# A hand-written order for TensorE beside the RWKV scan, and 16-wide diagonal blocks with two merges on TensorE

## The chip, the core and the metric

The kernel runs on one core of one Trainium2 chip. The metric is the device time of one execution in microseconds (us). The core has five engines that run side by side, each working through its own list in order: TensorE (PE, matrix products, with weight loads as PEld), VectorE (DVE), ScalarE (ACT), GpSimd (POOL) and SyncE (SP), which here only issues DMA transfers.

## The reference, cut to what matters

One encoder layer for two sequences (1024 and 256 tokens, width 1024): attention (MLA) and a bidirectional RWKV-7 scan side by side, merged by gates, then a SwiGLU FFN. What the change touches is the scan, the gates and the attention's output projection:

```python
def wkv_scan(r, w, k, v, kk, a, reverse):
    def step(S, inp):
        r_t, w_t, k_t, v_t, kk_t, a_t = inp
        sa = jnp.einsum('bhvk,bhk->bhv', S, -kk_t)
        S = (S * w_t[:, :, None, :]
             + sa[..., :, None] * (kk_t * a_t)[..., None, :]
             + v_t[..., :, None] * k_t[..., None, :])
        y = jnp.einsum('bhvk,bhk->bhv', S, r_t)
        return S, y
...
        o_mla = mla_branch(p_mla, q_a_norm[l], kv_a_norm[l], w_uq[l], w_ukv[l]) @ w_mla_o[l]
        o_rwkv = rwkv_branch(p_rwkv, ...) @ w_rwkv_o[l]
        gm, gr = jnp.split(jax.nn.sigmoid(p_gate), 2, axis=-1)
        x = x + g1 * ((gm * o_mla + gr * o_rwkv) @ w_out[l])
```

## The kernel before, in words

The scan is computed in chunks. A *batch* is 128 tokens of one sequence in both directions at once, with 8 heads: ten batches (two of the short sequence, eight of the long one). Inside a batch there are two *steps* of 64 tokens. Per step, direction and head a 64x64 triangular system has to be solved; its inverse is built once per batch for all 32 systems. The functions, in `phase_rwkv`:

- `front` and `left` make a batch's scaled keys `bk` and left factors `lt` on VectorE, ScalarE and GpSimd from tiles `ld` that SP loads.
- `prepare` runs four `part`s per batch: products `pA` (the triangular matrices and their partners), copies of them by ScalarE into `aa`, `lt` and `arb`, masks by GpSimd, transposes `pT` into `bkt`; then `value_rows` transposes the values (`pv`). The PSUM pool `pa` has three buffers.
- `invert` (called by `solve`) builds the inverses. Diagonal blocks of 32 are inverted on VectorE by a chain of 31 elimination steps with two instructions each (`xt`, L865, and `W`, L867), between transposes (`X` L856, `dt` L869, `xr` L871). Two products per block pair on TensorE (`pw`, L877 and L882), with copies `aa` (L878, L879) and `tt` (L884, L885) after each, merge the 32-blocks to 64.
- `step` is the serial part: products `py` (L913), copies `ru` (L916 on ScalarE, L917 on VectorE), `py` with the inverse `tt` (L919), copies `xv` (L920, L921), the state update `pS` (L925, L926), the outputs (L931) and their copies to `yt`.

Beside this chain `phase_fill` gives TensorE independent work, the *fill*: the gate products of nine column tiles over five 256-token pieces (weights from `w_in`, split into a high and a low half by `split_w`: ScalarE casts, GpSimd subtracts; kept in DRAM as `gw` for later pieces), and then the attention's output projection (`mla_out`). All its products are issued in `product` (L1041). Before, `phase_fill` was traced as a whole after the scan, and the compiler's scheduler set the order of every engine by priorities: a step's instructions lie 4000 places ahead of their place in the text (`HP`), a solve's 100 (`HI`), and where nothing of these was ready in its model of the time, fill went in. The order is fixed when the program is built; on the chip each engine follows it and waits where an operand is late.

After the scan, `join` and `merge` apply the scan's result (tile `or`, which takes the fill's buffer `x1`), and the FFN follows.

## Time and profile before

| | |
|---|---|
| time, median of 3 runs | 2687.57 us (2685.22 to 2699.12) |
| the profiled execution's own time | 2687.72 us |
| its span in the profile | 2686.0 us |
| TensorE / VectorE / ScalarE / GpSimd busy | 93% / 53% / 37% / 30% |
| mean granted clock of TensorE | 0.958 |

Busy shares are taken over the whole span. Instructions that only wait, issue DMAs or branch don't count as busy. The granted clock is a share of full speed: 1.00 is 2.4 GHz, 0.50 is 1.2 GHz. A product of f32 operands leaves two records in the profile, one in which the operands are fp32r leaves one.

### The profile page before, as it was taken

Reading aid. Unit: us, or ns where it says so; the run is one execution under the profiler, and the core shown is the slowest. Engines: PE = TensorE matmul, PEld = TensorE weight load, DVE = VectorE, ACT = ScalarE, POOL = GpSimd, SP = SyncE. Lnnn points to the kernel's source line nnn. Section 1 sums busy time; section 2 is a strip of 40 time slices with the busy share of each in tenths; the row PEclk is TensorE's granted clock in tenths of the full one; section 3 lists DMA queues with packets and bytes.
Section 4 is the critical chain, followed back from the end, with each engine's and each line's share of the span. In section 5 each row is a group of like instructions: output and inputs, shape, how many; then the busy total and the mean of one; then the engine's idle time right before and its main releaser. Section 6 shows DMA issues by size and latency. Waiting matters only on the chain.

```text
span 2686.0 us, 42442 instructions
## 1 busy us (share of the span) xinstructions
PE 2501.3 (93%) x17018; PEld 2121.5 (79%) x17018; DVE 1426.3 (53%) x2399; ACT 998.8 (37%) x1867; POOL 800.6 (30%) x789
## 2 busy tenths in 40 slices
PE   5999999989998799999898898899999999999997
PEld 3777777778887688888886677778888888888886
DVE  5655652357777688886785666552222232222328
ACT  4422332347676765555652233331110111101114
POOL 2112131021015655443434665442111111111123
PEclk7999999999999798899998999999999999999998
DMA  7654532100003545644656754221111111111113
GB/s 285 230 197 174 212 126 84 47 31 19 18 13 89 186 146 173 176 129 139 202 172 193 240 167 144 80 71 56 40 33 39 40 40 40 35 37 40 40 42 132
DMA packets 188470, 292.37 MB, mean 109 GB/s; under 512 B 16160, under 2 KB 106096, under 8 KB 188272
## 3 DMA queue, kind: packets, MB, share of 16 engines
q1 hardware_dynamic: 174880, 242.07, 28.4%
q0 software_dynamic: 5760, 26.22, 2.4%
q10 hardware_dynamic: 7632, 21.37, 2.3%
q8 instruction: 134, 2.20, 0.3%
q14 instruction: 64, 0.52, 0.1%
HBM read 211.95 MB, written 77.64 MB: 108 GB/s over the span
## 4 chain that ended last, share of the span: by engine, by line
PE 72%; DVE 16%; DMA 4%; issue 3%; POOL 2%; ACT 2%; SPq 0%; POOLq 0%; DVEq 0%; ACTq 0%
PE mm L67 43%; PE fp L1041 8%; PE s L627 3%; DVE xt L865 3%; DVE W L867 2%; PE o L661 2%; PE proj L560 2%; PE gps L453 2%; PE t L648 2%; PE pA L820 1%; PE py L913 1%; PE py L931 1%; PE ada_ps L170 1%; PE lora L369 1%; PE pS L925 1%
## 5 line engine op out<-in xcount | busy, mean ns | idle before, releaser
L55 POOL TENSOR_TENSOR wlo<-wraw,whi 128x1024 fp32r<-128x1024 f32 (+3 forms) x197 | 359.5, 1827 | 1168.0 <-ACT whi L53 1151.9
L53 ACT CAST whi<-wraw 128x1024 fp32r<-128x1024 f32 (+2 forms) x212 | 172.7, 818 | 917.3 <-issue 460.4
L67 PE MATMUL mm<-h2h,whi 128*128 128x512 f32 (+1 forms) x1056 | 279.5, 358 | 2.8 <-ACT whi L53 2.7
L67 PE MATMUL mm<-h2h,wlo 128*128 128x512 f32 (+1 forms) x1056 | 278.8, 358 | 2.7 <-POOL wlo L55 2.7
L67 PE MATMUL mm<-h2l,whi 128*128 128x512 f32 (+1 forms) x1056 | 278.3, 357 | 0.0
L67 PE MATMUL mm<-g,whi 128*128 128x512 f32 (+1 forms) x1056 | 240.7, 359 | 6.2 <-DVE ft L1251 5.6
L1041 PE MATMUL fp<-x,whi 128*128 128x256 f32 (+1 forms) x912 | 203.0, 316 | 15.0 <-ACT x L1023 8.3
L67 PEld LDWEIGHTS mm<-g,whi 128*128 128x128 f32 x1056 | 177.8, 190 | 38.0 <-issue 5.7
L67 PEld LDWEIGHTS mm<-h2h,whi 128*128 128x128 f32 x1056 | 177.2, 189 | 34.5 <-ACT whi L53 3.3
L67 PEld LDWEIGHTS mm<-h2h,wlo 128*128 128x128 f32 x1056 | 177.0, 189 | 34.3 <-POOL wlo L55 3.6
L67 PEld LDWEIGHTS mm<-h2l,whi 128*128 128x128 f32 x1056 | 177.1, 189 | 31.3 <-issue 0.5
L1263 DVE SCALAR_TENSOR_TENSOR x<-mm,g2h,x 128x512 f32<-128x512 f32 (+1 forms) x144 | 87.0, 656 | 196.3 <-PE mm L67 196.0
L1041 PEld LDWEIGHTS fp<-x,whi 128*128 128x128 f32 x912 | 153.5, 200 | 25.4 <-ACT x L1023 10.0
L1251 DVE SCALAR_TENSOR_TENSOR ft<-ft,mm 128x512 f32<-128x512 f32 (+1 forms) x66 | 36.0, 593 | 226.9 <-ACT ft L1250 226.9
L67 PE MATMUL mm<-hh,whi 128*128 128x512 f32 (+1 forms) x480 | 148.8, 368 | 6.9 <-ACT pp L320 3.9
L1041 PE MATMUL fp<-x,wlo 128*128 128x256 f32 (+1 forms) x456 | 144.4, 317 | 11.6 <-POOL wlo L55 7.6
L67 PE MATMUL mm<-hl,whi 128*128 128x512 f32 (+1 forms) x480 | 148.2, 365 | 7.0 <-DVE hl L265 6.9
L1252 DVE TENSOR_TENSOR ft<-ft,mm 128x512 f32<-128x512 f32 (+1 forms) x66 | 36.0, 593 | 217.5 <-PE mm L67 217.5
L67 PE MATMUL mm<-hh,wlo 128*128 128x512 f32 (+1 forms) x480 | 146.5, 365 | 0.0
L67 PE MATMUL mm<-g,wlo 128*128 128x512 f32 (+1 forms) x528 | 136.2, 359 | 1.2 <-POOL wlo L55 1.2
L865 DVE TENSOR_TENSOR xt<-W,X 128x126 f32<-128x126 f32 (+22 forms) x310 | 127.6, 412 | 9.0
L867 DVE TENSOR_TENSOR W<-W,xt 128x126 f32<-128x126 f32 (+22 forms) x310 | 125.0, 403 | 8.6
(320 smaller groups left out, 5210.7 us busy)
## 6 DMA issues: line engine op xcount, KB each, us to landing
wraw<-in_w_ffn_in_dram SPq DMA_DIRECT2D x56, 512.0 KB, 3.5
araw<-in_w_ada_dram ACTq DMA_DIRECT2D x32, 512.0 KB, 3.3
wraw<-in_w_ffn_out_dram SPq DMA_DIRECT2D x26, 512.0 KB, 3.6
wraw<-in_w_in_dram SPq DMA_DIRECT2D x20, 512.0 KB, 3.8
x<-scr_h SPq DMA_DIRECT2D x20, 512.0 KB, 7.7
whi<-scr_gw SPq DMA_DIRECT2D x36, 256.0 KB, 3.2
wlo<-scr_gw SPq DMA_DIRECT2D x36, 256.0 KB, 3.5
araw<-in_w_ada_dram SPq DMA_DIRECT2D x16, 512.0 KB, 9.4
```

Of the source, the lines that this page charges most:

```text
L53: nc.scalar.copy(hi, raw)
L55: (eng or nc.gpsimd).tensor_tensor(lo, raw, hi, ALU.subtract)
L67: nc.tensor.matmul(p[:, :n], lhsT=ww[:, k, :], rhs=aa[:, k, c0:c0 + n], start=(k == 0 and i == 0), stop=(k == kt - 1 and i == 2))
L453: nc.tensor.matmul(p[:, :n], lhsT=ww[:, k % 4, :], rhs=aa[:, k, c0:c0 + n], start=(k == 0 and i == 0), stop=(k == KT - 1 and i == 2))
L560: nc.tensor.matmul(p[:, :n], lhsT=ww[:, k, :], rhs=aa[:, k, c0:c0 + n], start=(k == 0 and i == 0), stop=(k == kt - 1 and i == 2))
L627: nc.tensor.matmul(s[:, o:o + w], lhsT=a[:, tt * P:(tt + 1) * P], rhs=b[:, c0 + o:c0 + o + w], start=(m == 0), stop=(m == 2))
L648: nc.tensor.transpose(t[:, j, :], prs[i][:, kk * P:(kk + 1) * P], g.ident)
L661: nc.tensor.matmul(o, lhsT=vs[h // 4][:, c0 // P + kk, h % 4, :], rhs=pts[j][m][kk // 4][:, kk % 4, :], start=(kk == 0 and m == 0), stop=( ...
L865: nc.vector.tensor_tensor(tv, W[:, h:, j:j + 1].broadcast_to([P, n, j]), X[:, j:j + 1, 0:j].broadcast_to([P, n, j]), ALU.mult)
L867: nc.vector.tensor_tensor(W[:, h:, 0:j], W[:, h:, 0:j], tv, ALU.add)
L1041: g.nc.tensor.matmul(p[:, c:c + n], lhsT=ww[:, k % 4, :], rhs=aa[:, k, :n], start=(k == 0 and i == 0), stop=(k == kt - 1 and i == 2))
L1263: nc.vector.scalar_tensor_tensor(x1[:, dt, c0:c0 + n], p[:, :n], g.g2h[:, dt, c0 // TP:c0 // TP + 1], x1[:, dt, c0:c0 + n], ALU.mult, ALU.add)
```

## The change

Four things change together.

1. **Order.** The loop over the batches now runs under a manual schedule for TensorE: its instructions are issued as the source has them. `phase_fill` has become a generator, which yields after each *unit* (one row tile of weights: 6 products of 256 columns, or 3), and `slot(n)` draws n units. Slots stand between nearly all groups of the scan. The other engines are still ordered by the scheduler.
2. **Fill.** `steps` replaces `product` here: it works k by k over both pieces, and at half of an item it issues the next item's weights. The projection runs over three pieces with a weight load each (24 in all) instead of two passes (16). Where the fill goes to other tokens, four units are skipped.
3. **Inverse.** VectorE eliminates only 16-wide blocks (15 steps of two instructions, on up to 64 elements). Two new groups of 64 products 32x16 (`pz`, L881 and L886), with a copy by ScalarE and an add by VectorE (L887), merge them to 32; the old merges to 64 (now L896 and L902) follow.
4. `sel` has two columns more, masks that pick the upper or lower 16 of each 32 partitions.

```diff
     def invert(aa, tt):
...
-        for j in range(31, 0, -1):
-            h = j // 2
-            n = 16 - h
...
+        for j in range(15, 0, -1):
+            n = 16 - j
+            tmp = rk.tile([P, 64], F32, tag="xt", name="xt", bufs=1)
             tv = tmp[:, 0:n * j].rearrange("p (i m) -> p i m", m=j)
...
+        xr = rk.tile([P, 2, 16, 16], F32, tag="ix", name="xr", bufs=1)
+        nc.vector.transpose(xr.rearrange("p t u m -> p m t u"), W.rearrange("p k (h m) -> p m h k", h=2))
+        we = rk.tile([P, 16, 32], F32, tag="iv", name="we", bufs=IB)
+        for t in range(2):
+            nc.vector.tensor_scalar(we[:, :, 16 * t:16 * t + 16], W[:, :, 0:16], g.sel[:, 2 + t:3 + t], None, ALU.mult)
+        dt = rk.tile([P, 16, 32], F32, tag="id", name="dt", bufs=IB)
+        nc.vector.transpose(dt.rearrange("p u (t k) -> p k t u", t=2), we.rearrange("p k (t u) -> p k t u", t=2))
+        pw = pa.tile([P, 16, 32], F32, tag="pa", name="pz")
+        for u in range(16):
+            for q in range(4):
+                nc.tensor.matmul(pw[G[q], u, 0:16], lhsT=aa[G[q], u, 0:32], rhs=xr[G[q], 0, u, :], start=True, stop=True)
+        nc.scalar.copy(W[:, :, 0:16], pw[:, :, 0:16])
+        slot(1, HI)
+        for u in range(16):
+            for q in range(4):
+                nc.tensor.matmul(pw[G[q], u, 16:32], lhsT=W[G[q], u, :], rhs=dt[G[q], u, 16:32], start=True, stop=True)
+        nc.vector.tensor_tensor(dt[:, :, 16:32], dt[:, :, 16:32], pw[:, :, 16:32], ALU.add)
         xr = rk.tile([P, 16, 32], F32, tag="ix", name="xr", bufs=1)
         nc.vector.transpose(xr, dt)
+        slot(2, HI)
...
-    def step(bt, sv, tt, st, last):
+    def slot(n, off=0):
+
+        with tc.high_priority(offset=-off):
+            for _ in range(n):
+                next(g.fill, None)
+
+    def step(bt, sv, tt, st, last, n):
...
+        slot(n[0], HP)
         for u, c, e, _, _, _ in ops:
             nc.tensor.matmul(py[e][HV[0], u, :], lhsT=tt[HV[e], 8 * st + u], rhs=ru[HV[e], c, :], start=(u == 0), stop=(u == 7))
...
+    with tc.manual_schedule(engines={mybir.EngineType.PE}):
+        bts[0] = prepare(0)
+        slot(8)
+        solve(0, bts[0])
+        bts[1] = prepare(1)
+        for i, (seq, b) in enumerate(batches):
+            cur = bts.pop(i)
+            with tc.high_priority(offset=HP):
+                begin(cur, svs[seq])
+                for st in range(2):
+                    step(cur, svs[seq], tts[i % TT], st, b == SEG[seq][1] // P - 1, (1, 2, 3) if i + 2 < nb else (2, 3, 5))
+            if i + 2 < nb:
+                bts[i + 2] = prepare(i + 2)
+            if i + 1 < nb:
+                solve(i + 1, bts[i + 1])
+                slot(1)
+        for _ in g.fill:
+            pass
...
+def steps(g, kt, parts, ws, half):
...
+    for k in range(kt):
+        wh, wl = ws[k // 4]
+        for i, (ww, e) in enumerate(((wh, 0), (wh, 1), (wl, 0))):
+            for p, a, n, first, last in todo:
+                g.nc.tensor.matmul(p, lhsT=ww[:, k % 4, :], rhs=a[e][:, k, :n], start=(k == 0 and i == 0 and first),
+                                   stop=(k == kt - 1 and i == 2 and last))
+        if k == kt // 2 - 1:
+            half()
+        yield
```

What stands in a row on the engines. First TensorE before, in the middle of a batch's first step: `fp` is fill, `py` and `pS` the step, `pA` and `pT` the preparation of the batch after the next.

```order
L1041 MATMUL fp<-x,whi 128x256 x2
L820 MATMUL pA<-lt,bk 128x128 x2
L925 MATMUL pS<-xv,bkt 64x64
L919 MATMUL py<-ru,tt_7622 64x64 x8
L925 MATMUL pS<-xv,bkt 64x64 x7
L931 MATMUL py<-xv,arb 64x64 x8
L820 MATMUL pA<-lt,bk 128x128 x6
L833 MATMUL pT<-cst,bk 128x128 x4
L1041 MATMUL fp<-x,wlo 128x256
L1041 MATMUL fp<-x,whi 128x256 x2
L925 MATMUL pS<-xv,bkt 64x64 x8
L931 MATMUL py<-xv,arb 64x64 x8
```

TensorE now, from the new merges to the inverse's last merge: `pz` are the new 16-wide merges, `pw` the old ones.

```order
L881 MATMUL pz<-xr,aa 32x16 x64
L1078 MATMUL fp<-x,whi 128x256 x4
L1078 MATMUL fp<-x,wlo 128x256 x2
L886 MATMUL pz<-dt,W 32x16 x64
L1078 MATMUL fp<-x,whi 128x256 x4
L1078 MATMUL fp<-x,wlo 128x256 x2
L1078 MATMUL fp<-x,whi 128x256 x4
L1078 MATMUL fp<-x,wlo 128x256 x2
L896 MATMUL pw<-xr,aa 32x32 x32
L1078 MATMUL fp<-x,whi 128x256 x4
L1078 MATMUL fp<-x,wlo 128x256 x2
L902 MATMUL pw<-dt,aa 32x32 x32
```

Preparation, steps and solve no longer lie in one another; each group is followed by one to three units of fill. One such unit, the step's L939, one unit, and L946 with the inverse follow the last row.

VectorE before, from the copy behind the last merge to the first step's copy `ru` (`xt` and `W` are the elimination of the next batch's blocks).

```order
L885 COPY tt_7622<-pw 32x16x32
L865 TENSOR_TENSOR xt<-W,X 128x31
L867 TENSOR_TENSOR W<-W,xt 128x31
L865 TENSOR_TENSOR xt<-W,X 128x30
L867 TENSOR_TENSOR W<-W,xt 128x30
L865 TENSOR_TENSOR xt<-W,X 128x58
L867 TENSOR_TENSOR W<-W,xt 128x2x29
L865 TENSOR_TENSOR xt<-W,X 128x56
L867 TENSOR_TENSOR W<-W,xt 128x2x28
L807 SCALAR_TENSOR_TENSOR lt<-ld,M 64x4x64 x2
L865 TENSOR_TENSOR xt<-W,X 128x81
L917 COPY ru<-py 64x512
```

VectorE now, the end of the same stretch; the rows ahead of these are the first 28 elimination instructions with the copies `aa` (L898) and `tt` (L905) among them, after the add L887, two L807 and the transpose L889.

```order
L867 TENSOR_TENSOR xt<-W,Y 128x15
L869 TENSOR_TENSOR W<-W,xt 128x15
L872 STREAM_TRANSPOSE xr<-W 128x16x32
L875 TENSOR_SCALAR we<-W,sel 128x16x16 x2
L807 SCALAR_TENSOR_TENSOR lt<-ld,M 64x4x64 x2
L943 COPY ru<-py 64x512
L807 SCALAR_TENSOR_TENSOR lt<-ld,M 64x4x64 x2
L877 STREAM_TRANSPOSE dt<-we 128x16x2x16
L948 COPY xv<-py 64x8x64
```

Before, the copy `ru` stood behind nine of the 62 elimination instructions that follow a merge; now it stands behind all 30.

## Rows read from the trace of the kernel before

**Rows 1.** The page: span, and busy time of two engines.

```profile
span 2686.0 us, 42442 instructions
...
PE 2501.3 (93%) x17018; PEld 2121.5 (79%) x17018; DVE 1426.3 (53%) x2399; ACT 998.8 (37%) x1867; POOL 800.6 (30%) x789
```

**Rows 2.** Windows: length, busy PE, PEld, DVE, ACT, POOL, then PEclk, DMA share, GB/s.

```profile
871.70:1503.70 632.00, 566.47 (x6682) 512.60 (x6680) 462.92 (x978) 348.83 (x758) 283.53 (x383) 0.91 0.56 171
871.70:930.00 58.30, 41.53 (x282) 36.75 (x281) 40.48 (x85) 38.95 (x93) 36.41 (x56) 0.77 0.62 194
930.00:1395.00 465.00, 432.58 (x5599) 399.89 (x5598) 361.74 (x778) 278.25 (x612) 208.12 (x296) 0.93 0.53 162
1395.00:1503.70 108.70, 92.36 (x807) 75.96 (x805) 60.70 (x116) 31.63 (x55) 39.00 (x32) 0.92 0.63 196
1503.70:2686.00 1182.30, 1130.90 (x5720) 950.13 (x5720) 439.45 (x654) 243.48 (x395) 337.54 (x186) 0.98 0.22 69
```

**Rows 3.** Waits of PE from 855 to 1500: us in total, times, longest.

```profile
PE py L919 <- DVE ru L917: 12.2, 10, 4.4
PE pA L820 <- ACT arb L829: 9.1, 3, 8.2
```

**Rows 4.** Windows of 1 us, PE alone: length, busy, PEclk, DMA share, GB/s.

```profile
1195.00:1196.00 1.00, 0.00 (x0) 1.00 1.00 312
...
1199.00:1200.00 1.00, 1.00 (x10) 0.50 0.00 0
...
1206.00:1207.00 1.00, 1.00 (x23) 1.00 0.00 0
```

**Rows 5.** Timeline of PE from 1163.8: start, us, line, operation, records.

```profile
1163.82 1.20 PE L882 MATMUL pw<-dt,aa 32*32 32x32 f32 x64
1164.95 0.38 PE L1041 MATMUL fp<-x,wlo 128*128 128x256 f32 x1
1165.17 0.40 PE L1041 MATMUL fp<-x,whi 128*128 128x256 f32 x2
1165.41 0.28 PE L1041 MATMUL fp<-x,wlo 128*128 128x256 f32 x1
...
1167.05 0.33 PE L919 MATMUL py<-ru,tt 64*64 64x64 f32 x2
```

**Rows 6.** Timeline of PE in the last step, two records per product.

```profile
1473.63 3.77 PE L913 MATMUL py<-xv,lt 128*64 128x64 f32 x64
...
1481.24 1.90 PE L919 MATMUL py<-ru,tt 64*64 64x64 f32 x32
```

**Rows 7.** The start: PE's first `pA`, SP's loads of `x`, their landing.

```profile
871.77 1.16 PE L820 MATMUL pA<-lt,bk 64*128 64x128 f32 x16
...
873.22 7.46 SPq L1132 DMA_DIRECT2D x<-scr_h  x8
...
DMA to landing us min/median/max: 6.0/9.1/9.8
```

**Rows 8.** Groups of DVE by form, 890 to 1450: busy us, mean ns, idle before.

```profile
L807 DVE SCALAR_TENSOR_TENSOR lt<-ld,M 64x256 f32<-64x256 f32 x68 | 41.9, 616 | 4.7 <-DMA ld<-scr_kk 1.9 <-PE py L913 1.8
L917 DVE COPY ru<-py 64x512 f32<-64x512 f32 x18 | 12.3, 683 | 0.5
L867 DVE TENSOR_TENSOR W<-W,xt 128x56 f32<-128x56 f32 x20 | 7.6, 382 | 0.6
L871 DVE STREAM_TRANSPOSE xr<-dt 128x512 f32<-128x512 f32 x10 | 7.1, 710 | 0.3
L879 DVE COPY aa<-pw 32x512 f32<-32x512 f32 x10 | 7.0, 697 | 46.4 <-ACT aa L878 46.3
L865 DVE TENSOR_TENSOR xt<-W,X 128x16 f32<-128x16 f32 x10 | 1.8, 181 | 0.3
```

**Rows 9.** Group of PE, 1440 to 1720: products on `or`, idle before and releasers.

```profile
L1041 PE MATMUL fp<-or,whi 128*128 128x512 f32 (+1 forms) x192 | 54.4, 376 | 6.5 <-DVE gt L1102 3.0 <-DVE or L1024 2.3 <-ACT or L1023 1.2
```

More of the change, by code (lines that the diff above doesn't have):

```diff
@@ L1000, in phase_rwkv @@
     nb = len(batches)
-    bts[0] = prepare(0)
-    solve(0, bts[0])
-    bts[1] = prepare(1)
-    for i, (seq, b) in enumerate(batches):
-        cur = bts.pop(i)
-        with tc.high_priority(offset=HP):
-            begin(cur, svs[seq])
-            for st in range(2):
-                step(cur, svs[seq], tts[i % TT], st, b == SEG[seq][1] // P - 1)
-        if i + 2 < nb:
-            bts[i + 2] = prepare(i + 2)
-        if i + 1 < nb:
-            solve(i + 1, bts[i + 1])
+    with tc.manual_schedule(engines={mybir.EngineType.PE}):
[16 more added lines that the diff above has]
+            pass
     def join(c0, out):
@@ L1173, in scaled @@
             split_in(g, raw, a[0][:, j, :], a[1][:, j, :])
-    def mla_out(*parts):
-        for dt in range(KT):
-            ts = [row("gt", n) for _, _, n in parts]
-            for t, (_, c0, n) in zip(ts, parts):
-                nc.sync.dma_start(out=t, in_=g.scr["gate"][dt, :, c0:c0 + n])
-            for p, t, (_, c0, n) in zip(product(g, io["w_mla_o"][dt], 4, [[(a, n)] for a, _, n in parts]), ts, parts):
-                nc.vector.scalar_tensor_tensor(t, t, 1.0, p, ALU.add, ALU.mult)
-                nc.sync.dma_start(out=g.scr["xm"][dt, :, c0:c0 + n], in_=t)
@@ new lines, in phase_fill, with half @@
+    box = [items[0][2]()]
+    xs, on = [load(i, c0) for i, c0 in enumerate(spans[0])], 0
+    ahead = {}
+    for at, (j, s, _) in enumerate(items):
+        if s != on:
+            if s < 3:
+                xs = [load(i, c0) for i, c0 in enumerate(spans[s])]
+            if s in (1, 2):
+                yield from [None] * 4
+            if s == 2:
+                ahead[3] = scaled(pair(1, 4, 512), *CH[0])
+            if s >= 3:
+                xs = [ahead[s]]
+                if s < 5:
+                    ahead[s + 1] = scaled(pair((0, 1)[s - 3], 4, CH[s - 2][1]), *CH[s - 2])
+            on = s
+        def half(at=at):
+            if at + 1 < len(items):
+                box.append(items[at + 1][2]())
+        n, c0 = sum(x[1] for x in xs), xs[0][2]
+        t = row("gt", n)
+        if s >= 3:
+            nc.sync.dma_start(out=t, in_=g.scr["gate"][j, :, c0:c0 + n])
+        p, = yield from steps(g, KT if s < 3 else 4, [[x[:2] for x in xs]], box.pop(0), half)
+        if s < 3:
+            nc.scalar.activation(t, p, AF.Tanh, scale=0.5)
+            nc.sync.dma_start(out=g.scr["gate"][j, :, c0:c0 + n], in_=t)
+        else:
+            nc.vector.scalar_tensor_tensor(t, t, 1.0, p, ALU.add, ALU.mult)
+            nc.sync.dma_start(out=g.scr["xm"][j, :, c0:c0 + n], in_=t)
```

77 lines of the change are left out of this document (37 added, 40 removed).

## The prediction

> **What bounds the kernel now.** I read the page first: TensorE is busy in 93% of the span and VectorE in 53% [rows 1], so a faster VectorE is worth something only where TensorE stands still for it. The change touches one stage, from the first `pA` product to the first product on `or` (871.7 to 1503.7 us). The windows over that stage [rows 2] split its 632 us: TensorE is busy 566, so it stands still 66; its granted clock averages 0.91, so (1 - 0.91) x 632 = 57 us more are lost to the half clock. What is left, 566 - 57 = 509 us, is work at full clock. The three parts show where the losses lie: the first 58 us lose 17 to standing and about 13 to the clock, the middle 465 lose 32 and 33, the end 16 and 9. After 1503.7 the clock is 0.98 and no edit reaches.
>
> So the stage is TensorE's own work for four fifths, and at most 123 us can be won in it. The list of TensorE's waits [rows 3] says for whom it stands: for the copy `ru` on VectorE 12.2 us in ten waits, for `arb` on ScalarE 9.1. VectorE is late because each batch's 62 elimination steps run between the copies. The clock follows the standing: from 1195 to 1196 TensorE did nothing at all, at 1199 it ran at 0.50 (1.2 GHz of the two levels, 1.2 and 2.4), and only at 1206 at 1.00 (2.4 GHz) again, though it was busy with scan products all that time [rows 4]; a wait is paid twice.
>
> **What the change takes and adds, on TensorE.** The old fill and scan products stay. Ten solves each get two groups `pz` of 64 products 32x16 (L881, L886). The nearest row is the old merge: 32 products 32x32 (64 records) start at 1163.82 and the next product at 1164.95, so 1.13 us, 35 ns each [rows 5]. If issue sets that, a group takes 64 x 35 = 2.3 us (call it 2.4); if it is the columns and the quarters of the array in use (half the columns, four quarters instead of two), 0.6. I take 1.8, nearer the row, as the instruction count is what certainly doubles: 10 x 2 x 1.8 = 36 us (12 to 48).
>
> The Trainium skill bears on this in two ways that disagree. "TensorEngine Tiling (Array Packing)", Gotcha 1: PSUM Pressure, says that different row tiles can't access the same PSUM bank at once; all four quarters of `pz` write one bank, and by that rule the sum would take the 48. "TensorE: Matmul & The Clock Gate", Part 3: Packing small matmuls, says that products in different row groups run concurrently; by that rule it would take the 12. The old merge alternates two row groups in one bank, and its 35 ns are less than half of the 118 that a 64-column product takes (32 in 3.77 us [rows 6]), so the first rule isn't borne out in full, nor the second shown.
>
> The fill now comes in units of 6 products of 256 columns between nearly all scan groups. Sixteen such products took 2.10 us from 1164.95 to 1167.05, where two in the steady run take 0.24 (1165.17 to 1165.41); 16 x 0.12 = 1.9, so 0.2 us go to entering and leaving a block [rows 5]. Counted in the order, this stage had 88 fill blocks and now has 175: 87 x 0.2 = 17 us (none, if the switches between scan groups that fall away save as much). Work: 509 + 36 + 17 = 562.
>
> **Where the new order waits.** *Start, 13 + 4.* The first fill unit now stands behind the first `pA` (1.16 us from 871.77, so over at 872.9 [rows 7]) and everything else behind it. Its data are the seventh DMA of SP's order; before, eight were issued in 7.46 us from 873.2 and landed 6.0 to 9.8 us later [rows 7], so about 880 + 6 = 886: TensorE stands 13 us, where before it did the first batch's `pA` and `pT` in that time. Then the first elimination chain (about 12 us) has some 8 us of fill and transposes over it: 4 more.
>
> *Solve and first step, 45.* This is the term that decides. By the order shown, VectorE does between the end of the second `pz` group and the copy `ru` of the next step: the add L887 (not in the trace; 0.45, between the small steps and L917's 0.68), four L807 at 0.616, the transposes L889 at 0.71 and L872 at about 0.9, the copies L898 and L905 at 0.70, two L875 at about 0.3, `ru` at 0.683: 7.2 us [rows 8]. Among them stand all 30 steps of the *next* batch's elimination. A 16-element step took 0.181, a 56-element one 0.382 [rows 8] beside GpSimd's work, which here too follows at once (the `lt` products L811); the new steps have 15 to 64 elements, I take 0.30: 9 us (5.4 to 11.5). So VectorE needs 16.2 us (12.6 to 18.7). TensorE has for that time a slot of two units (1.6), two merges (1.13 each), two slots of one (0.9 each), L939 (3.7, as L913 before), one more slot and half of L946 (0.95, as L919): 11.2 us [rows 5, 6]. It stands 5.0 (1.4 to 7.5) in each of nine batches: 45 us (13 to 67). Behind the waiting L946 are the state update, both steps and the next batch's preparation, so nothing else fills it.
>
> *Others.* In `prepare`, ScalarE's copies free the PSUM that the next `pA` needs; before, that wait cost 9.1 us [rows 3] and the order could put fill there; with only one or two units to cover it, 10. The second load of `x` (same eight DMAs, the sixth of them needed) has four skipped units and some 10 us of scan over it: 4. The last batch has hardly any fill left: 6. A whole wait for DMA on a gate weight is possible, but in the new order a half is fetched four units ahead; nothing for it.
>
> Standing: 13 + 4 + 45 + 10 + 4 + 6 = 82. The half clock: 3 at the start, 2 at the load, 1 per solve, since a cold TensorE lets VectorE catch up: 14 of the 57 remain. Stage: 562 + 82 + 14 = 658 against 632, **+26 us**. At its end `or` is ready early now, while before the first products on it waited 2.3 + 1.2 us [rows 9]: -4. The half of VectorE's elimination that falls away (62 steps to 30) is hidden: it runs under TensorE's work unless `ru` waits for it. The 8 more weight splits and the wider `sel` are under it too. With the profiled execution's 2687.7 us (1.7 around the span; the median is the same): 2687.7 + 22 = **2710**.
>
> **Rivals.**
> *It is faster: the chain is short.* Steps at 0.19 us uncontended put the solve's standing at 13 to 15 us in all; `pz` takes 12; evenly spread fill keeps the clock up (8 lost). With 37 for the other standing, 509 + 12 + 17 + 37 + 15 + 8 = 598, less 4: 38 us faster, 2650. For it speaks that the clock fell after standing only, and that VectorE loses half its load; against it, that the small steps took up to twice that beside GpSimd. It decides below 2.6 us of standing per solve (22 us over nine).
> *It is cold throughout.* The solve's two waits of several us lie among tiny products; if the clock then stays at 0.50 into the steps in every batch (41 us lost, against 57 before), with `pz` at 48 and the chain at 67: 509 + 48 + 17 + 37 + 67 + 41 = 719, less 4: 83 slower, 2771.
> *It cancels.* The stage is TensorE's work, and what is taken from standing and clock (123 us before) comes back as 53 of work and 70 of new waits: 2688. That needs one term less than I think, a solve wait of 2.6 or `pz` at 14.
>
> **Chances.** Forecast 0.46 (2680 to 2736 by its own terms), faster rival 0.30, cold rival 0.14, cancelling 0.10. About 0.5%, 13 us, is what a measurement of this kernel can tell from no change. Of the forecast 0.13 lies within that, of the faster rival 0.02: faster 0.28, same 0.25, slower 0.47. The range goes from the one rival to the other, 2650 to 2770, since the steps' contention, `pz` and the clock are unknown both ways.
>
> **What would show it.** Right: in the waits after, L946 on `ru` (L943) leads with about 5 us per batch; `pz` groups of 1.2 to 2.4 us; the first fill product near 886; idle in the stage at 80, the clock above 0.91. Wrong: `ru` under 2 us per batch and VectorE's small steps near 0.2; or a granted clock that falls in each solve; or a wait that I gave nothing, on gate or `w_mla_o` weights.

## The result and the profile after

The changed kernel takes 2780.05 us (median of 4 runs, 2772.72 to 2781.34) against 2691.52 of the kernel before beside it: 1.0322 times as long, 95% interval 1.0286 to 1.0358. It is 88 us slower; 22 were forecast, and 2780 lies 10 above the range.

The page of the changed kernel, the rows that answer to [rows 1]:

```profile
span 2777.2 us, 47359 instructions
...
PE 2525.2 (91%) x19578; PEld 2139.5 (77%) x19578; DVE 1292.6 (47%) x2138; ACT 1009.9 (36%) x1885; POOL 801.3 (29%) x796
```

VectorE lost 134 us of work, as it should. The windows of the changed kernel over the same stage, first `pA` to first product on `or`, whole and in three parts, and what follows (columns as in [rows 2]):

```profile
871.50:1599.90 728.40, 594.80 (x9242) 533.10 (x9241) 328.09 (x718) 360.18 (x776) 284.83 (x391) 0.84 0.50 152
871.50:930.00 58.50, 30.05 (x246) 27.39 (x249) 21.32 (x49) 25.14 (x58) 28.14 (x39) 0.73 0.69 227
930.00:1502.00 572.00, 481.72 (x7459) 431.74 (x7452) 257.55 (x571) 292.71 (x637) 223.13 (x317) 0.85 0.50 151
1502.00:1599.90 97.90, 83.04 (x1554) 73.96 (x1552) 49.23 (x99) 42.34 (x82) 33.56 (x36) 0.86 0.37 113
1599.90:2777.20 1177.30, 1126.32 (x5721) 947.55 (x5720) 440.39 (x652) 243.33 (x394) 336.02 (x186) 0.98 0.21 70
```

All of it is in the stage: 728.4 us against 632.0 [rows 2], while the rest is 5 shorter. TensorE's busy time rose by 28 only; it stands 133.6 us instead of 65.5, most of the rise in the middle part (90 for 32), and the clock averages 0.84 instead of 0.91. TensorE's waits in the stage (us in total, times, longest):

```profile
PE fp L1078 <- DMA x<-scr_h: 25.7, 7, 8.5
PE pw L902 <- DVE aa L898: 18.3, 9, 4.2
PE pw L896 <- DVE xr L889: 17.5, 5, 9.1
PE pz L886 <- ACT W L882: 16.8, 8, 2.9
PE pz L881 <- DVE xr L872: 10.1, 1, 10.1
PE py L946 <- DVE ru L943: 8.3, 4, 4.3
PE pw L896 <- DVE xt L867: 7.1, 2, 4.3
PE pA L820 <- ACT arb L829: 5.1, 5, 3.0
```

The wait on `ru`, which was to lead with 45, has 8.3. The hand-overs inside the solve have more: `W` 16.8, `xr` 17.5 (and 7.1 that name `xt`, the next instruction of VectorE), `aa` 18.3, and 10.1 before the very first group. One solve shows how. TensorE, timeline (start, us, line; two records per product, "[ ]" is the idle time before and its releaser):

```profile
1157.90 1.58 PE L881 MATMUL pz<-xr,aa 32*32 32x16 f32 x128
1159.41 0.74 PE L1078 MATMUL fp<-x,whi 128*128 128x256 f32 x4
...
1162.66 1.26 PE L886 MATMUL pz<-dt,W 32*32 32x16 f32 x128 [2.26 <-ACT W L882]
1163.85 0.79 PE L1078 MATMUL fp<-x,whi 128*128 128x256 f32 x4
...
1169.22 1.92 PE L896 MATMUL pw<-xr,aa 32*32 32x32 f32 x64 [2.88 <-DVE xt L867]
```

ScalarE and VectorE in the same solve:

```profile
1157.87 3.01 ACT L846 COPY xv<-pv 64x256 f32<-64x256 f32 x8
1161.48 0.63 ACT L782 ACTIVATE E<-M 128x512 f32<-128x512 f32 x1 [0.59 <-DVE M L780]
1162.01 0.20 ACT L786 ACTIVATE f<-f 128x12 f32<-128x12 f32 x1
1162.23 0.37 ACT L882 COPY W<-pz 128x256 f32<-128x256 f32 x1
```

```profile
1164.05 0.42 DVE L887 TENSOR_TENSOR dt<-dt,pz 128x256 f32<-128x256 f32 x1 [2.45 <-PE pz L886]
1167.57 0.85 DVE L807 SCALAR_TENSOR_TENSOR lt<-ld,M 64x256 f32<-64x256 f32 x2 [3.11 <-DMA ld<-scr_kk]
1168.46 0.71 DVE L889 STREAM_TRANSPOSE xr<-dt 128x512 f32<-128x512 f32 x1
```

The copy `W` takes 0.37 us but stands on ScalarE behind eight copies of `pv`, 3.0 us, and behind two instructions for a later batch (L782, L786), the first of which waits 0.59 for VectorE. The transpose `xr` takes 0.71 but stands behind L807 of the next preparation, which waits 3.1 us for the load of `kk`. Over the first TensorE has one unit of fill (1.0 us), over the second two (2.5 us, most of it at half clock). And the clock, windows of 1 us of TensorE (length, busy, granted clock, DMA share, GB/s):

```profile
1163.00:1164.00 1.00, 1.00 (x110) 1.00 0.17 49
1165.00:1166.00 1.00, 1.00 (x7) 0.50 0.74 207
1177.00:1178.00 1.00, 1.00 (x13) 0.50 0.00 0
1178.00:1179.00 1.00, 1.00 (x22) 0.97 0.00 0
```

After the wait on `W` it fell at about 1164.5 to 0.50 and stayed there to 1178, through a second wait (2.9 us, on `xr`), both old merges and into the step's first products.

**A better split of the stage.** The prediction took (1 - granted clock) times the stage as lost, which counts time in which TensorE stood as well, and takes a product at 0.50 for twice as long. The changed kernel's timeline of TensorE says what it is:

```profile
909.43 0.64 PE L1078 MATMUL fp<-x,whi 128*128 128x256 f32 x4
909.91 0.40 PE L1078 MATMUL fp<-x,wlo 128*128 128x256 f32 x2
...
933.08 1.91 PE L886 MATMUL pz<-dt,W 32*32 32x16 f32 x128
...
975.09 1.06 PE L1078 MATMUL fp<-x,whi 128*128 128x256 f32 x4
975.94 0.63 PE L1078 MATMUL fp<-x,wlo 128*128 128x256 f32 x2
```

The 64 `pz` products at 933.08 (clock 0.50) took 1.91 us and those at 1162.66 (1.00) 1.26, 1.5 times; four fill products took 0.85 us from 975.09 to 975.94 at 0.50 and 0.48 from 909.43 to 909.91 at 1.00, 1.8 times. With 1.7 between, 0.41 of the busy time at half clock is lost. The busy time at half clock is summed over windows of 1 us. "Work" is busy time less that loss.

| stage | us | work | lost to half clock (busy at half) | standing | ratio to before (interval) |
|---|---|---|---|---|---|
| before | 632.0 | 526 | 40 (98.5) | 65.5 | |
| changed | 728.4 | 531 | 64 (155.3) | 133.6 | 1.0322 (1.0286 to 1.0358) |
| e1 old blocks in the new order and fill | 694.2 | 507 | 57 (138.9) | 129.8 | 1.0224 (1.0207 to 1.0241) |
| e2 new blocks alone | 675.4 | 574 | 58 (142.2) | 42.7 | 1.0159 (1.0131 to 1.0186) |
| e13 scheduler's order | 706.8 | 577 | 78 (189.2) | 52.5 | 1.0290 (1.0266 to 1.0313) |
| e3 more fill in the solve | 740.9 | 542 | 50 (120.8) | 149.1 | 1.0395 (1.0379 to 1.0411) |
| e4 late elimination | 732.4 | 531 | 72 (175.8) | 129.5 | 1.0351 (1.0336 to 1.0367) |
| e5 sixth `ld` buffer | 728.2 | 531 | 70 (170.4) | 127.0 | 1.0341 (1.0316 to 1.0365) |
| e6 products in the waits | 746.4 | 599 | 42 (101.7) | 105.4 | 1.0391 (1.0369 to 1.0414) |
| e14 fill later alone | 724.1 | 530 | 63 (152.6) | 131.4 | 1.0381 (1.0353 to 1.0409) |
| e7 solve inside preparation | 681.5 | 528 | 47 (115.2) | 106.4 | 1.0172 (1.0146 to 1.0198) |
| e8 inside and late | 713.6 | 524 | 53 (129.2) | 136.8 | 1.0271 (1.0245 to 1.0297) |
| e9 one part earlier | 664.2 | 525 | 40 (98.5) | 98.7 | 1.0098 (1.0073 to 1.0122) |
| e10 and fill later | 659.7 | 524 | 47 (115.5) | 88.5 | 1.0038 (1.0023 to 1.0053) |
| e11 old blocks inside | 664.3 | 501 | 48 (116.2) | 115.5 | 1.0106 (1.0079 to 1.0134) |
| e12 values after second part | 684.6 | 530 | 55 (134.2) | 99.9 | 1.0151 (1.0127 to 1.0176) |
| e15 first solve later | 663.3 | 527 | 46 (111.3) | 91.1 | 1.0099 (1.0078 to 1.0120) |
| e16 fill in the steps | 653.8 | 529 | 40 (98.2) | 84.2 | 1.0068 (1.0049 to 1.0087) |

So the 96 us of the stage are +5 of work, +24 of half clock and +68 of standing. The columns up to standing come from one profiled execution each, the ratios from four to ten executions. Executions of one kernel differ by up to 16 us (e10: 2691.78 to 2707.72), and what follows the stage took between 1174.8 us (e10) and 1188.2 (e14) in these profiles though none of the runs is about it. A difference of some 10 us between two rows, or one that the ratio shows and the stage does not, is therefore not explained here.

### The profile page after: what moved, and what is told of

Same layout as the page of the kernel before. It is cut to its first block, busy times and chain, and to the rows that moved or that the text cites. A ratio compares the mean times of both kernels' runs of the same rounds, so it can differ in the third digit from the quotient of the medians.

```text
span 2777.2 us, 47359 instructions
## 1 busy us (share of the span) xinstructions
PE 2525.2 (91%) x19578; PEld 2139.5 (77%) x19578; DVE 1292.6 (47%) x2138; ACT 1009.9 (36%) x1885; POOL 801.3 (29%) x796
## 4 chain that ended last, share of the span: by engine, by line
PE 72%; DVE 12%; DMA 6%; ACT 3%; issue 3%; POOL 3%; SPq 1%; POOLq 0%; DVEq 0%; ACTq 0%
PE mm L67 42%; PE fp L1078 5%; PE fp L1096 3%; PE s L627 3%; PE o L661 2%; PE py L939 2%; PE gps L453 2%; PE proj L560 2%; PE t L648 2%; PE pA L820 1%; PE py L959 1%; DMA ld<-scr_kk 1%; PE py L946 1%; DVE xt L867 1%; PE pS L953 1%
## 5 line engine op out<-in xcount | busy, mean ns | idle before, releaser
L55 POOL TENSOR_TENSOR wlo<-wraw,whi 128x512 fp32r<-128x512 f32 (+3 forms) x205 | 370.2, 1807 | 1196.5 <-ACT whi L53 1175.8
L1078 PE MATMUL fp<-x,whi 128*128 128x256 f32 (+1 forms) x912 | 210.9, 344 | 26.3 <-DMA x<-scr_h 25.7
L1078 PEld LDWEIGHTS fp<-x,whi 128*128 128x128 f32 x912 | 145.9, 210 | 41.1 <-issue 14.5
L1078 PE MATMUL fp<-x,wlo 128*128 128x256 f32 (+1 forms) x456 | 123.3, 324 | 3.4 <-POOL wlo L55 3.1
L627 PE MATMUL s<-kb,q 128*128 128x512 f32 (+1 forms) x432 | 111.6, 391 | 2.3 <-ACT pr L633 2.2
L67 PEld LDWEIGHTS mm<-hh,whi 128*128 128x128 f32 x480 | 85.0, 192 | 28.3 <-issue 6.9
```

Source lines behind the costliest of these rows:

```text
L55: (eng or nc.gpsimd).tensor_tensor(lo, raw, hi, ALU.subtract)
L67: nc.tensor.matmul(p[:, :n], lhsT=ww[:, k, :], rhs=aa[:, k, c0:c0 + n], start=(k == 0 and i == 0), stop=(k == kt - 1 and i == 2))
L627: nc.tensor.matmul(s[:, o:o + w], lhsT=a[:, tt * P:(tt + 1) * P], rhs=b[:, c0 + o:c0 + o + w], start=(m == 0), stop=(m == 2))
L1078: g.nc.tensor.matmul(p, lhsT=ww[:, k % 4, :], rhs=a[e][:, k, :n], start=(k == 0 and i == 0 and first), stop=(k == kt - 1 and i == 2 and last))
```

## The experiments

Times are compared by their ratio to the kernel before beside them; 0.01 is 27 us.

### Taking the change apart

**e1.** The old `invert` in the changed kernel, with its two merges alone; the slots of the solve become 3 and 1 units.

```diff
-        for j in range(15, 0, -1):
+        for j in range(31, 0, -1):
...
+        slot(3, HI)
         pw = pyp.tile([P, 16, 32], F32, tag="py", name="pw")
```

> The hand-written order and the fill in units stay, the inverse goes back to 32-wide elimination on VectorE (62 steps) with only the two old merges; the slot of one unit between the two new groups is put ahead of the first old merge, so that the fill per batch is the same. Theory A (the round trips between TensorE and VectorE or ScalarE inside the solve, covered by only one or two units, cost the time, once as standing and once more as half clock): two round trips fewer, but VectorE's 62 steps stand among the rest, so still 40 to 90 slower than before, about 2750. Theory B (the hand-written order is the loss whatever the inverse is): as the changed kernel, 2770 to 2790. Theory C (the new products on TensorE are the loss): near before, 2690 to 2705.

Measured 1.0224, 60 us slower than before, as theory A had it. The waits moved to other copies (`xr` 24.3, `aa` 15.3, `tt` 13.6, `ru` 9.5), and the standing of the stage is nearly the same, 129.8 for 133.6. TensorE's work is 19 *less* than before. Groups of TensorE over the stage, before, and below the same in e1 (busy us, mean ns, idle before):

```profile
L820 PE MATMUL pA<-lt,bk 64*128 64x128 f32 x640 | 81.6, 313 | 13.9 <-ACT arb L829 9.1 <-issue 2.6 <-ACT lt L827 0.8
L925 PE MATMUL pS<-xv,bkt 128*64 128x64 f32 x576 | 46.9, 247 | 2.7 <-DVE xv L921 2.6
```

```profile
L820 PE MATMUL pA<-lt,bk 64*128 64x128 f32 x632 | 58.9, 309 | 22.4 <-ACT arb L829 11.3 <-issue 6.2 <-POOL bk L789 4.2
L937 PE MATMUL pS<-xv,bkt 128*64 128x64 f32 x576 | 37.7, 231 | 1.2 <-DVE xv L932 1.1
```

The same products take 23 and 9 us less in unbroken groups than cut up among each other, though TensorE then stands 8.5 us more ahead of `pA`.

**e2.** The new `invert`, `W` and `sel` in the kernel before; no slots, the old fill.

```diff
-        for j in range(31, 0, -1):
+        for j in range(15, 0, -1):
...
+        pw = pa.tile([P, 16, 32], F32, tag="pa", name="pz")
```

> The 16-wide blocks with their two new groups on TensorE, in the kernel before: the scheduler's order, the old fill. The new groups took 1.25 us each at full clock in the changed kernel, 25 us for twenty. Theory A: the scheduler can put any fill between the merges, so only the products' own time comes on top, 2690 to 2715. Theory B: no loss at all, 2680 to 2700, as VectorE has half its elimination less. Theory C: 2740 to 2780.

Measured 1.0159, 43 us slower, between theories A and C. Standing falls to 42.7, the least of all; work rises by 48 and half clock by 18. The groups:

```profile
L879 PE MATMUL pz<-xr,aa 32*32 32x16 f32 x1280 | 22.6, 192 | 6.8 <-DVE xr L870 6.8
L892 PE MATMUL pw<-xr,aa 32*32 32x32 f32 x640 | 18.1, 193 | 0.0
L883 PE MATMUL pz<-dt,W 32*32 32x16 f32 x1280 | 17.2, 185 | 2.1 <-issue 2.1
L897 PE MATMUL pw<-dt,aa 32*32 32x32 f32 x640 | 13.7, 192 | 0.7 <-DVE aa L894 0.7
```

Cut up by the scheduler, `pz` costs 40 here (31 in the changed kernel) and the old merges 32 (26 before). The wait on VectorE's `ru` did fall, from 12.2 to 1.4, but VectorE had time to spare before, so what the blocks save there is worth little: they bought 23 us of standing for 48 of work.

**e13.** The changed kernel without manual schedule and slots.

```diff
-    with tc.manual_schedule(engines={mybir.EngineType.PE}):
+    with ExitStack():
...
-            for _ in range(n):
-                next(g.fill, None)
+        return
```

> The changed kernel with the order given back to the scheduler: no manual schedule, no slots, and the new fill (units, both pieces k by k, the projection over three pieces, the skipped steps without effect) is drawn whole behind the scan's text. If the hand-written order is what costs (theory A with its gaps): as the run with the blocks alone, 2725 to 2745. If the fill's new form costs (three passes of the projection's weights, a load of x for every change of tokens, products that share no run of columns): 15 to 50 above that run, 2750 to 2780.

Measured 1.0290: the fill's new form costs 35 us over e2, and the order by hand only 9 on top of that, which the intervals don't tell from nothing. Against e2 it is 20 of half clock, 10 of standing and 3 of work; why the clock is low for longer with this fill is settled only in part (the last section). From e13 to the changed kernel, which is the hand-written order alone: work -46, half clock -14, standing +81, together 22 in the stage.

### Taking single waits out of the changed kernel

**e3.** Seven more units in the solve, fewer in the preparation.

```diff
-        slot(2 - st)
+        slot(1)
...
-        slot(2, HI)
+        slot(4, HI)
```

> The changed kernel with the slots inside the solve at 3, 4, 4 units instead of 1, 2, 1, and those in the preparation at 1 and 1 instead of 2 and 2 or 1, so nearly the same fill per batch. Standing in the solve was 73 us in ten batches by the waits on W, xr and aa, and the fill units take 0.71 us. Theory A: seven units more (5 us) cover most of 7 us of waits per batch, and the clock stays up for longer: 30 to 60 faster than the changed kernel, 2720 to 2750, with up to 10 lost in the preparation on ScalarE's copies. Theory B (the many small blocks cost, wherever they stand) and C: within 8 us of the changed kernel, 2772 to 2788.

Measured 1.0395, slower than the changed kernel: against all three theories. Waits of TensorE in e3:

```profile
PE pw L896 <- DVE xr L889: 20.6, 5, 7.2
...
PE pA L820 <- ACT arb L829: 13.4, 16, 1.2
...
PE pv L843 <- ACT arb L829: 10.3, 14, 1.0
```

`W` and `aa` fell to 7.0 and 9.7, but the preparation now waits for ScalarE, and `xr` hardly fell (20.6, against 24.6 with the 7.1 on `xt`). Fill is too scarce to be had twice.

**e4.** `X` takes the buffer of `ru`, so that the elimination stands behind both steps.

```diff
-        X = rk.tile([P, 16, 32], F32, tag="iv", name="X", bufs=IB)
+        X = rk.tile([P, 16, 32], F32, tag="ru", name="X", bufs=1)
```

> The changed kernel, where the transposed blocks X take the buffer of the copy ru instead of one of their own. The elimination of the next batch can then only begin when the second step has read its ru, so in VectorE's order all its steps stand behind the steps and ahead of the next merges; TensorE's order is unchanged. Theory A1 (within A: VectorE's elimination, which stands among the merges' copies, makes them late): the waits on aa (18 us), on ru (8) and part of those on xr (25) go, with the half clock behind them: 30 to 50 faster than the changed kernel, 2730 to 2750. Theory A2 (within A: the bare round trips cost, the elimination is not in their way): 0 to 12 faster. Theory C: no change.

Measured 1.0351, not faster. The waits on `aa` (12.6) and `ru` (0.6) fell as theory A1 had it, those on `W` (21.4) and `xr` (22.6 and, for the first group, 19.4) did not: `W` rose by 4.6, the first group by 9.3, and `xr` had 24.6 with `xt` before.

**e5.** A sixth `ld` buffer.

```diff
-LT, LDB, EB, YB, BK, HP, HI, IB, TT = 5, 5, 4, 1, 2, 4000, 100, 1, 2
+LT, LDB, EB, YB, BK, HP, HI, IB, TT = 5, 6, 4, 1, 2, 4000, 100, 1, 2
...
-        Y = rk.tile([P, 16, 16], F32, tag="iy", name="Y", bufs=IB)
+        Y = X[:, :, 0:16]
```

> The changed kernel with six buffers instead of five for the tiles ld that the scan's preparation loads; to make room, the masked blocks Y are written in place over X. TensorE's order is unchanged. In the changed kernel VectorE's L807 stands ahead of the transpose xr (L889) and waited 34 us in eight waits for the load of kk, which was issued late, when a buffer of ld had come free. Theory D (what makes the solve late is work of the next batch's preparation ahead of its copies, and that work waits for its loads): kk is loaded earlier, the waits of TensorE on xr (25 us) fall by 10 to 20 and the half clock behind them by 5 to 10: 15 to 30 faster than the changed kernel, 2750 to 2765. Theory A2 (the bare round trips): within 6 of it.

Measured 1.0341. Its waits:

```profile
PE pw L902 <- DVE aa L898: 27.8, 10, 7.2
...
PE pw L896 <- DVE xr L889: 5.3, 2, 4.9
```

The wait on `xr` fell from 17.5 to 5.3, and what it had covered came up behind it, at `aa` (18.3 to 27.8) and `ru` (8.3 to 12.3). Theory D was right on the load and wrong on its worth.

**e6.** Products that nothing reads, behind the solve's slots.

```diff
+    def warm(n):
+        pk = psp.tile([P, 3, P], F32, tag="ps", name="wm")
+        for _ in range(n):
+            nc.tensor.matmul(pk, lhsT=g.ident, rhs=g.cst, start=True, stop=True)
...
         slot(2, HI)
+        warm(4)
```

> The changed kernel with products that nothing reads (128x384 of constants) behind the slots inside the solve: three behind the first new group, four behind the second, three behind the first old merge. In the changed kernel TensorE stood 73 us at these places and did 155 us of its stage at half clock, against 98 before. A 128-column product of f32 takes about 0.15 us, so one of these takes about 0.45 to 0.65 at full clock and ten some 5 to 6.5 per batch, 50 to 65 in all, less than the standing there. Theory E (the clock falls for the standing, and that is a good third of the loss): the standing in the solve is filled with work, the clock stays up, 25 to 45 faster than the changed kernel though TensorE does more, 2735 to 2755. If the clock has no part in it: 0 to 25 slower, as the new products overshoot some of the waits.

Measured 1.0391, 19 slower than the changed kernel, the time expected if the clock had no part. The group of these products:

```profile
L859 PE MATMUL wm<-cst 128*128 128x384 f32 x200 | 80.5, 547 | 1.2 <-issue 1.2
```

They took 80 us, more than estimated, and removed only 28 of standing. The clock did stay up: busy time at half clock fell from 155 to 102, worth 22 us by the split. So in the hand-written order the half clock hangs on the standing in the solve, as theory E says, but what comes back is a fourth of the loss, not a third, and dummy work is dearer than it.

**e14.** Skipped units alone.

```diff
+    yield from [None] * 10
...
-                yield from [None] * 4
+                yield from [None] * 8
```

> The changed kernel with the skipped units alone: ten at the start and eight instead of four at the later changes of tokens; the solve stays where it is. TensorE stood 26 us for the loads of x there. If that standing is a loss of its own, whatever the solve does: 10 to 20 faster than the changed kernel, 2760 to 2770. If it only paid where the solve was covered: within 6 of the changed kernel.

Measured 1.0381; its interval overlaps the changed kernel's. The waits on the loads of `x` fell from 25.7 to 9.7, and the first group of `pz` waited 15.0 instead of 10.1. Where the solve stands uncovered, a wait taken out is found again: the standing of the stage is 131.4 for 133.6. The stage is 4 us shorter; that the time is longer, by the ratios 16, comes from behind the stage (1188.2 for 1177.3 us in the profiles) and is not explained.

### Giving the solve other work

**e7.** The four groups of the solve, one behind each part of the next preparation.

```diff
                 part(o, st, bt.aa)
+                go()
...
-                bts[i + 2] = prepare(i + 2)
-            if i + 1 < nb:
-                solve(i + 1, bts[i + 1])
+                bts[i + 2] = prepare(i + 2, go)
```

> The changed kernel, where the four groups of products of the inverse stand one behind each of the four parts of the preparation of the batch after, instead of all four behind one another after it; their fill units go with them, and the new groups take PSUM from the pool of the steps. Between two of them TensorE then has a part (1.2 + 0.6 us) and three to four units, some 4 to 5 us, instead of one or two units. Theory A (the round trips inside the solve, uncovered, cost the time): of 73 us of standing there 40 to 60 go and 10 to 20 of half clock, 50 to 80 faster than the changed kernel, 2700 to 2730. Theory B (hand-written order as such): no change, 2770 to 2790.

Measured 1.0172: 40 us faster than the changed kernel by the ratios, where 50 to 80 were expected. Waits of TensorE in e7:

```profile
PE py L943 <- DVE tt L909: 28.8, 8, 6.2
...
PE py L950 <- DVE ru L947: 13.2, 9, 4.1
...
PE pw L906 <- DVE aa L901: 0.5, 1, 0.5
```

The waits on `W`, `xr` and `aa` inside the solve are gone (`aa` 18.3 to 0.5); 9.1 ahead of the second `pz` group have no releaser in the profile, and part came up at the end of the solve, `tt`, behind the elimination. The edit also moves the PSUM of `pz` to the pool of the steps, which was not run by itself; ahead of `pA` and `pv`, which keep the old pool, TensorE stood 9 us less than in the changed kernel (4.8 for 14.1), so that is the most standing that the pool can have saved.

**e8.** e7 with e4's edit.

> As the run with the solve inside the preparation, and with the elimination held back as in the run on late elimination (X in the buffer of ru). If the elimination stands in the way of the copies ru and tt there: 5 to 20 faster than that run. If the first new group then waits for its elimination, or the products lt of the next batch stand ahead of ru instead: 0 to 15 slower than that run.

Measured 1.0271: the first group of each solve now waits for its elimination, 51.5 us for `xr` of L872. A miss on size: 27 slower, not 15.

**e9.** e7 with each group one part earlier, and the elimination behind the first step's `ru`.

```diff
-        X = rk.tile([P, 16, 32], F32, tag="iv", name="X", bufs=IB)
+        X = rk.tile([P, 16, 32], F32, tag="ru", name="X", bufs=1)
...
         go()
+        go()
...
-        ru = rk.tile([P, 8, 64], F32, tag="ru", name="ru", bufs=1)
+        ru = rk.tile([P, 8, 64], F32, tag=("ru", "iv")[st], name="ru", bufs=1)
```

> As the run with the solve inside the preparation, but each of its four groups stands one part earlier (the first ahead of the first part), so that the last copy tt has a whole part and pv over it; and the elimination begins when the first step has read its ru (X in the buffer of that ru, the second step's ru in another), so that it lies beside the steps and not in front of the first ru and xv. In that run TensorE stood 29 us for tt, 13 for ru and 8 for xv. If the place of VectorE's copies among its elimination is what is left of the loss (theory A): 35 or so of these 50 go, with some half clock, 30 to 45 faster than that run, 2700 to 2715. If the standing only moves to the next copy, as it did with the sixth buffer: within 10 of it, 2735 to 2755.

Measured 1.0098, 20 us better than e7; 30 to 45 were expected. `tt` is gone from the waits, `ru` has 4.9 on VectorE and 11.0 on ScalarE. Half clock is back at the level of before.

**e10.** e9 with e14's skipped units.

> As the run with the solve one part earlier, and where the fill changes to other tokens more units are skipped: ten at the start (none before) and eight instead of four later. TensorE stood 18 to 26 us for the loads of x in all the runs with the hand-written order. If that standing is a loss of its own: 10 to 20 faster than the run without the skipped units. If the scan's own gaps, then without fill, take its place: within 6 of it.

Measured 1.0038 (1.0023 to 1.0053), 16 better than e9, as expected: the waits on `x` fell from 18.3 to 3.3, and here 10 of these 15 stayed gone (standing 98.7 to 88.5). In the profiles only 4.5 of it lies in the stage, since 7 more are lost to half clock. The windows of e10 over its stage:

```profile
871.50:1531.20 659.70, 571.28 (x9242) 517.43 (x9241) 316.23 (x715) 359.54 (x774) 283.02 (x390) 0.89 0.55 165
```

Together e7, e9 and e10 bring back 76 of the 87 us (by the stage, 69 of 96) with the same products and the same fill: only the places differ, with the PSUM pool of `pz` and the buffers of `X` and the second `ru`.

### Towards a faster kernel

**e11**, e10 with the old blocks:

> As the run with skipped units, but with the old 32-wide elimination on VectorE and its two merges alone, one behind the first part of the preparation and one behind the second; the elimination takes what place the scheduler gives it. The new groups of products cost 31 us of TensorE's time in the changed kernel. If the 16-wide blocks are no help once the solve is covered: 15 to 30 faster than the run with skipped units, near or below the kernel before, 2670 to 2695. If VectorE's 62 steps then stand in front of the copies again: slower than that run, 2710 to 2740.

Measured 1.0106. Work is 23 less (501), but VectorE's 62 steps stand in front of `ru` (22.8 us) again, and standing is 27 more.

**e12**, e10 with `pv` behind the second part and one unit more in each step:

> As the run with the solve one part earlier and the skipped units, with two moves more: the transposes pv and ScalarE's eight copies of them stand behind the second part of the preparation instead of at its end, and one unit of fill per step goes from the preparation into the first gap of each step (2, 2, 3 instead of 1, 2, 3; one instead of two behind the first two parts' pT). In that run TensorE still stood 17 us for ru, 13 of it for ScalarE, whose copies of pv (3.0 us) stand ahead of it, and the preparation of the next batch began at the end of this one's, when pv gave its buffers back. If that standing is of the same kind (a copy behind other work of its engine, with too little of TensorE's over it): 8 to 20 faster than that run, 2682 to 2694, which is the kernel before. If the parts behind the moved copies then wait for ScalarE instead: within 6 of that run.

Measured 1.0151, a miss. The wait on `ru` fell from 17 to 5, but `pA` waits 16.9 for the moved copies and `pS` 21.4 for `xv`.

**e15**, e10 with the very first solve one part later:

> As the run with the solve one part earlier and the skipped units, but in the very first solve the four groups stand one part later again, behind the first part of the second batch's preparation. In that run TensorE stood 15 us at the start for the first elimination. If that standing is a loss of its own: 5 to 12 faster than that run, 2690 to 2698. If the start is bounded by ScalarE's copies or the load of x instead: within 5 of it.

Measured 1.0099, 16 slower than e10, a miss too by its time: the first group still waits 10.7 and the step 14.5 for `xv`. The stage is only 4 longer.

**e16**, e15 with e12's unit in the steps alone:

> As the run with the first solve later, and one unit of fill per step moved from the preparation into the step's first gap (2, 2, 3 and one behind each pT), without the move of pv that the run on the values had besides. If the move of pv was what made that run 31 slower: this one is 0 to 8 faster than the run with the first solve later, as the wait on ru (17 us) goes. If it was the missing fill in the preparation: 15 to 30 slower.

Measured 1.0068, 8 better than e15 (the intervals touch) and 22 better than e12, so in e12 the move of `pv` did the harm. No version beats the kernel before; e10 comes within about 10 us. By its stage e16 is the shortest of the hand-written ones (653.8 against 659.7 in e10), by its time 8 longer than e10, so which of the two is better stays open.

## Why the prediction was wrong, point by point

**The sum.** +26 in the stage were 53 of work, 16 of standing and -43 of half clock. Measured by the better split: +5, +68, +24; by the prediction's own count, which takes all time at half clock as lost, -31, +68, +59. By either count work was put too high, standing and half clock too low. The -4 at the end met a 5, but not for its reason alone: the waits on `or` (2.3 + 1.2) are gone, those of the same products on `wlo` rose from 3.7 to 6.6, and what follows the stage varies by 13 us between these profiles.

**Standing: the step that failed is "Solve and first step, 45".** It set VectorE's 16.2 us from the end of the second `pz` group to `ru` against TensorE's 11.2 in the same stretch and took the difference, standing at `ru`. But in that stretch the two engines meet three times, at `xr`, `aa` and `ru`, and slack at one meeting can't be used at the next: `xr` and `aa` come later than the one or two units ahead of them last. The hand-over ahead of the stretch, `W` on ScalarE, had no term. And VectorE isn't at work all the time: L807 waited 34 us in eight waits for the load of `kk`. Measured are 71 us in the ten solves: 18 at `W` (16.8, and 1.5 of issue), which were given nothing, and 53 in the stretch itself (17.5 + 7.1 at `xr`, 18.3 at `aa`, 8.3 + 1.5 at `ru`). That 53 is near 45 is luck, since four fifths of it stand at meetings that the term did not have. That the place of the solve is the cause of them is shown by e7 and e9, which give it other work over it; that no single one of these waits is, by e4 and e5, in which it only moved.

The price of the elimination itself was right: in the solve shown, steps of 0.13 to 0.23 us but for one of 0.59, 0.25 with what lies between, so 7.5 us for 30 against 9. Of its own signs of being wrong, `ru` under 2 us per batch with steps near 0.2 came true, though by its rivals little standing there was to mean a faster kernel; the clock that falls in the solves came true as well.

The smaller terms: the loads of `x` at the start 15.0 (13 forecast), the first elimination 10.1 (4), the second load 6.7 (4), a third load 4.1 that was given nothing, the preparation about 16 on `arb`, `bk` and `bkt`, 3.8 of it without a releaser (10).

**Half clock: "1 per solve, since a cold TensorE lets VectorE catch up".** This step failed by more. One solve had 14 us at 0.50 in the rows above, and VectorE did not use them to catch up where TensorE next stood: 2.9 us for `xr`, already at half clock, while VectorE itself waited for `kk`. Only behind that, at `aa` and `ru`, TensorE found its operands ready. The term forecast 43 us less than before and measured 24 more, a miss of 67, the largest of the three; by the prediction's own count it is 116 us for 14. The cold rival, at 2771 with 0.14, named this mechanism and came nearest in time, but by luck: by that count it had 574 of work for 478, 104 of standing for 134 and 41 of half clock, less than the 57 before, for 116.

**Work.** `pz` was right: 36 forecast, 31 by its groups (14.2 + 16.9), which at full clock would be 24 (1.19 us from 1162.66 to 1163.85, times 20). A product takes 18.6 ns there, where the old merge took 35 [rows 5]: with half the columns and four row groups in one bank instead of two, half as long; which of the two makes it shorter no run separates. By the Trainium skill, "TensorEngine Tiling (Array Packing)", Gotcha 1: PSUM Pressure, different row tiles can't access one PSUM bank at once, which the prediction put at 2.4 us a group; by the Trainium skill, "TensorE: Matmul & The Clock Gate", Part 3: Packing small matmuls, products in different row groups run at the same time, which it put at 0.6. The measured 1.19 lies between and nearer the second. The 17 us for 87 more fill blocks had the wrong sign: what a block costs at its ends is less than what the scan's own groups lost by being cut up among each other. e1 has 19 us less work than before with the same units, and from e13 to the changed kernel the hand-written order saves 46. Counted in the timelines, TensorE goes from one group to another 360 times in the stage before, 520 in e2, 553 in e13 and 389 in the changed kernel.

**What the change is worth by its parts.** The blocks alone cost 43, since they move work from an engine that had time onto the one that bounds the stage. The fill's new form costs 35 in the scheduler's order, most of it at half clock; this part I can't trace to a wait, and most of it stays open. The hand-written order by itself won 46 of work and 14 of half clock and lost 81 of standing: 22 us in the stage, 9 in the time, where the intervals overlap.

## What to carry to other kernels

Where two engines hand work back and forth, price each hand-over by itself (what stands ahead of the copy on its engine, and how much independent work the first engine has over it), not the chain by its ends: standing doesn't add up to a difference of sums. A hand-written order needs independent work at every hand-over, and the best there is may be another part of the chain itself rather than fill: moving four groups of products among the preparation and the elimination beside the steps (e7, e9) was worth 60 us with no product saved. And taking one wait out of such a chain was worth nothing here as long as the next one stood right behind it (e4, e5).

## What the chip showed that was not expected

The granted clock can stay at half for long while TensorE does nothing but work. In e2 it stood from about 1205.3 to 1208.5; windows of TensorE (columns as above):

```profile
1207.00:1208.00 1.00, 0.00 (x0) 1.00 0.65 182
...
1238.00:1239.00 1.00, 1.00 (x22) 1.00 0.63 236
```

```profile
1210.00:1237.00 27.00, 27.00 (x345) 0.50 0.20 58
```

For 27 us after a wait of 3.2 us it was busy throughout, with steps, `pz`, `pA` and fill, at 1.2 GHz, before 2.4 came back at 1237. In the changed kernel it was 14 us after a wait of 2.3, with the second wait in them. By the split that is 11 us lost behind a wait of 3.2. A wait's second price can be several times its first, and it falls after the wait, on products that waited for nothing.

The clock also falls without a wait. Seven microseconds later in e2, TensorE having been busy without a gap since 1208.5 (columns as in [rows 2]):

```profile
1242.39 0.81 PE L892 MATMUL pw<-xr,aa 32*32 32x32 f32 x38
```

```profile
1244.00:1245.00 1.00, 1.00 (x7) 1.00 (x6) 0.94 (x3) 0.00 (x0) 0.00 (x0) 0.50 0.00 0
```

Before it fell, TensorE had done `pw` products cut up among `pA`, and then fill. By the profiles this happened five times in the stage of e2 (17 us at 0.50) and eight times in that of e13 (34 us), each time with no standing in the 12 us before and with `pz` or `pw` products among `pA`, `pT` or `pv` just ahead. Before the change, in the changed kernel and in e1, e6, e9 and e10 it did not happen: each fall had 1.0 us or more of standing in the 12 us before it. So "the clock follows the standing" holds for the kernels that it was read from and not for the new blocks in the scheduler's order, where the least standing (42.7) goes with more half clock than before; and 17 of the 47 us by which e13 is busier at half clock than e2 are of this kind. What in these products lets the clock fall no run separates.

The Trainium skill, "TensorE: Matmul & The Clock Gate", "Loop structure matters more than you think", has VectorE's copy out of PSUM as harmless for the clock where the next products follow at once. Here the products had to wait for such copies, and the clock fell: 1.2 us for VectorE's `ru` up to 1467.29 in the changed kernel, with 0.50 from about 1468.2; the waits above were for copies by ScalarE (`W` in the changed kernel, `ru` in e2).
